# SSD and z with tokens on the partitions, decay exponents from one matmul, the norm by 128 tokens

## The chip, the cores and the metric

One core of a Trainium2 chip runs the whole kernel. The metric is the device time of one execution in microseconds (us). PE is the matrix engine, DVE the vector engine, ACT the scalar engine, POOL GpSimd, SP the engine whose queue issues most DMAs. The matrix engine's granted clock has two levels here, 1.2 and 2.4 GHz (0.50 and 1.00 in the profile).

## What is computed

One layer of a decoder for a prompt of 2048 tokens and 8 samples of 4 tokens, 1024 channels wide. The normed input goes through one projection; four groups of 256 channels (S5, attention, SSD, short convolution) work on its parts; each is normed, all four go through W_out, and a feed-forward net follows. The change is in the SSD group and in its gate z:

```python
def ssd_scan(x, a, bm, cm, h0):
    ...
    acum = jnp.cumsum(jnp.transpose(a.reshape(bsz, nc, chunk, H), (0, 3, 1, 2)), axis=-1)
    li = jnp.arange(chunk)
    lmat = jnp.exp(jnp.where(li[:, None] >= li[None, :],
                             acum[..., :, None] - acum[..., None, :], -jnp.inf))
    scores = jnp.einsum('bclhn,bcshn->bhcls', ch, bh) * lmat
    y_diag = jnp.einsum('bhcls,bcshp->bclhp', scores, xc)
    decay_states = jnp.exp(acum[..., -1:] - acum)
    states = jnp.einsum('bclhn,bhcl,bclhp->bchpn', bh, decay_states, xc)
    ...
    y_off = jnp.einsum('bclhn,bchpn,bhcl->bclhp', ch, new_states[:, :-1], jnp.exp(acum))
...
    y = y + d_skip.astype(F32)[:, None] * xs
    y = y.reshape(bsz, T, SSD_WIDTH).astype(z.dtype) * jax.nn.silu(z)
    return rmsnorm(y, norm_g), h_new, new_buf
```

The prompt has 16 chunks of 128 tokens, 4 heads of 64 channels, 2 groups of B and C, and a state of 128.

## The kernel before

**Stages.** The norm of the inputs and the first projections come first, then the dense products of the input projection with S5 and the samples' attention beside them (to 811 us). SSD's products with X follow from 838 to 1017 us, the products with W_out (`px<-w,cat`) from 1053 to 1310 us, and the feed-forward net takes the rest. The prompt's attention runs as filler beside the end of the dense part, SSD and W_out; its last product with V is at 1195.7 us.

**Order.** A scheduler fixes each engine's instructions in one row when the program is built; at run time an engine takes its row strictly in order. What is traced at an earlier priority is taken first where it is ready, so `run` traces SSD ahead of the attention, and the attention ahead of W_out. Tiles come from pools: a name with `bufs=n` has n slots, handed out in the order in which the program is traced, and a slot is free again when its last reader is done.

**Input projection.** `w_cols` lists the chunks of 128 columns in their order. `dense_xbc` makes xBC (6 chunks) and z (2 chunks, last) with channels on the partitions: for each chunk and block of 512 tokens `proj_feat` issues 24 products of 512 columns; `proj_tok` is its counterpart with tokens on the partitions, 24 products of 128 columns for each 128 tokens and chunk. Both go through `silu2` to `xbcD` in DRAM, 8 rows of channels.

**SSD.** `prepare(i)` makes what does not wait for the state: it loads `sxbc` (every second chunk) and `sac`, the cumulated log decays as a row for each head read by all partitions (L1058). It transposes x and B (`px<-cst,sxbc`), makes `sX`, `sXd`, `sBt`, two exponentials (`seA` L1071, `sE` L1076), where four DVE operations (L1075) subtract the column's sum, G = B C, its mask (`sGm` L1081), `sE` times `sGm` (L1085), and `sCe` on POOL (L1087). `advance(i)` makes y with channels on the partitions (`pd<-sE,sX`, `pd<-sCe,shT`), the state (`px<-sXd,sBt`, L1106, L1107), the skip by D (L1110) and the gate (L1112). `feat_norm_out` norms 256 tokens at once: squares (L983), sums by a product with ones, rsqrt, product back to all partitions, scale (L995), split to two fp16 parts in `cat`. The samples' SSD (`sample`) and the preparation of W_out's weights (`wo`, `w_out`, L171 and L178) are steps of the same loop.

**Attention.** For each block of 512 queries (j) and head, `attend` makes scores (`pb<-k,q`, `pb<-kbm,q`), an exponential to `P` (L874), two fp16 parts `ph` (L878) and `pl` (L881), and products with V (`pb<-v,ph`, `pb<-v,pl`); the maxima of scores are found ahead (L843). After four heads `fox_out` norms 128 tokens at a time: squares with the sum (L928) into `fo_ssq`, rsqrt on POOL (L145, L146) into `fo_rs`, scale (L931), two transposes (`pb<-cst,fo_on`), split (L465, L466), DMA to `cat`. A block's output `fo_o` has one buffer:

```python
                o = f1.tile([128, 4, 256], F32, name="fo_o")
...
        ssq = self.col("fo_ssq", bufs=4)
...
        rs = self.col("fo_rs", bufs=4)
```

`col` takes these two from the pool `small`, which the whole kernel shares.

Of the kernel before, what the change touches and what calls it, by code (L numbers as in the profile page):

```python
# [9 lines left out]
F32 = mybir.dt.float32  # L10
# [3 lines left out]
AF = mybir.ActivationFunctionType  # L14
# [3 lines left out]
T = 2048          # prompt tokens  # L18
NT = 16           # prompt token tiles
D = 1024  # L20
KT = 8
B = 8             # sample batches
TS = 4            # sample tokens per batch
# [4 lines left out]
BLOCKS = [(2, 3), (0, 1)]  # blocks of 512 tokens, by pass over the FFN's weights; the first pass takes the samples too  # L28
FC = 256          # hidden channels of a step of the FFN
PLAIN = ((0, 15), (1, 15))      # (pass, step) of the FFN that leave the vector engine to others: products down as they come  # L30
V_EARLY, V_LAG = 12, 4     # token tiles whose v is made beside the norm of the inputs, and how far behind it
# [5 lines left out]
def host_constants():  # L37
# [17 lines left out]
    # score rows (head, batch, token); pages on partitions (batch % 4, page)  # L55
# [8 lines left out]
    # rows (token group, batch parity, head, token) of the products with V  # L64
# [4 lines left out]
    c["m8"] = (r[:, None] - 64) // 2 == np.arange(4)[None, :]  # L69
    offs, cols, n = {}, [], 0  # L70
# [8 lines left out]
    return offs, np.ascontiguousarray(np.concatenate(cols, 1)), n0  # L79


C_OFFS, C_ARR, C_LATE = host_constants()
# [16 lines left out]
class K:  # L99
    """One step of the hybrid trunk on one core."""  # L100
# [9 lines left out]
    # ------------------------------------------------------------ helpers  # L110
# [6 lines left out]
    @contextmanager  # L117
    def banks(self, **tags):
        """the group of PSUM banks (x, d or b) that a tag stands for"""
        old, self.bank = self.bank, tags  # L120
        yield
        self.bank = old

    @contextmanager
    def priority(self, p):
        """the scheduler takes what is traced here as if it were traced at p"""
# [14 lines left out]
    def rsqrt(self, out, v, add, mul):  # L141
        """out = (v * mul + add) ** -0.5 on small tiles"""
# [5 lines left out]
    def pow2(self, out, v):  # L148
        """the power of two at or below v > 0"""
# [8 lines left out]
    def wprep(self, loads, kt, ncols, tag="w", st=None):  # L158
        """Load weights, scale them by a power of two that bounds the chunk's norm by 2**15,
        split into fp16 parts.  Returns tile [128, kt, 2, ncols], scale, 1/scale."""  # L160
# [8 lines left out]
    def split(self, hi, lo, x, sc):  # L169
        """fp16 parts of sc * x"""  # L170
# [3 lines left out]
    def wscale(self, st, junk, sc, inv, top):  # L174
        """the power of two that brings the norm of st to 2**top or below, and its inverse"""
# [2088 lines left out]
```

## Time and profile before

| what | value |
| --- | --- |
| runs | 2616.5, 2621.11, 2626.45 us; median 2621.11 us |
| profiled execution | span 2617.2 us, 50130 instructions |
| PE busy | 2431.6 us (93%) |
| DVE busy | 2050.2 us (78%) |
| ACT busy | 1308.3 us (50%) |
| POOL busy | 1246.8 us (48%) |

The span is the time from the first to the last recorded instruction of one profiled execution, and stands 3.9 us under the median of the runs. Shares are means over stages with different limits; they are read stage by stage below.

### The profile page before, as it was taken

How to read it: one execution, taken by the hardware profiler on the slowest of the kernel's cores; microseconds unless marked ns; L12 is line 12 of the kernel's file. 1: busy time of each engine (PE TensorE's matmuls, PEld its weight loads, DVE VectorE, ACT ScalarE, POOL GpSimd, SP SyncE). 2: the span in 40 equal slices, each digit the busy share in tenths (PEclk: the TensorE clock that was granted, in tenths of full speed). 3: DMA queues.
4: the chain of work that ended last, by engine and by line, in shares of the span. 5: the costliest groups of instructions: out<-in, count | busy, mean ns of one | idle time of the engine just before them, and what ended most of it. 6: DMA issues, size and time to landing. Idle time of an engine off the chain costs nothing.

```text
span 2617.2 us, 50130 instructions
## 1 busy us (share of the span) xinstructions
PE 2431.6 (93%) x19944; PEld 1628.7 (62%) x19944; DVE 2050.2 (78%) x3822; ACT 1308.3 (50%) x2376; POOL 1246.8 (48%) x1274
## 2 busy tenths in 40 slices
PE   6989999999988898999969999999998999999997
PEld 5875554444444666778956666666665666666664
DVE  5666667875565988665579998899998898999996
ACT  6444332033335566565365655655556554455554
POOL 3503122223113766454265565556656666666652
PEclk9999999999998989999989999999999999999999
DMA  6333416869724343436111121111126211121211
GB/s 189 93 75 93 90 38 215 305 253 331 229 84 149 109 136 96 129 108 227 52 41 49 49 65 49 49 49 49 62 81 232 96 49 49 65 65 49 65 33 65
DMA packets 205476, 282.27 MB, mean 108 GB/s; under 512 B 33765, under 2 KB 170082, under 8 KB 194970
## 3 DMA queue, kind: packets, MB, share of 16 engines
q1 hardware_dynamic: 195866, 211.44, 25.8%
q0 software_dynamic: 9376, 67.64, 7.1%
q8 instruction: 156, 2.56, 0.4%
q14 instruction: 78, 0.64, 0.1%
HBM read 221.90 MB, written 54.28 MB: 106 GB/s over the span
## 4 chain that ended last, share of the span: by engine, by line
PE 29%; DVE 12%; POOL 12%; ACT 5%; issue 3%; DMA 3%; POOLq 0%; DVEq 0%; ACTq 0%
PE pb L135 17%; PE px L135 11%; DVE x L2150 3%; DVE wu L172 2%; DMA ws<-in_w_up_dram 2%; DVE wd L172 1%; POOL ws L1996 1%; ACT wu L171 1%; POOL ws L1995 1%; POOL ws L1998 1%; POOL ws L1997 1%; ACT wd L171 1%; POOL ws L2022 1%; POOL ws L2024 1%; ACT wdT L171 1%
## 5 line engine op out<-in xcount | busy, mean ns | idle before, releaser
L135 PEld LDWEIGHTS <-wu 128*128 128x128 f16 x5376 | 528.9, 99 | 229.6 <-issue 43.4
L2150 DVE SCALAR_TENSOR_TENSOR x<-pb,ff,x 128x512 f32<-128x512 f32 x840 | 592.0, 740 | 26.5 <-PE pb L135 22.7
L135 PE MATMUL px<-hn,wu 128*128 128x256 f16 (+1 forms) x3072 | 427.6, 276 | 20.4 <-ACT fr L2057 10.0
L135 PE MATMUL px<-xT,w 128*128 128x512 f16 (+1 forms) x2160 | 416.3, 343 | 2.4 <-ACT da L721 2.1
L135 PEld LDWEIGHTS <-ht 128*128 128x128 f16 x2712 | 264.0, 98 | 226.4 <-issue 25.8
L135 PE MATMUL pb<-wdT,ht 128*128 128x512 f16 x1440 | 376.7, 379 | 10.4 <-DVE x L2150 8.1
L135 PE MATMUL pb<-wd,ht 128*128 128x512 f16 x1272 | 334.8, 379 | 10.4 <-DVE x L2150 10.4
L135 PE MATMUL pb<-hn,wu 128*128 128x256 f16 (+1 forms) x2304 | 302.1, 277 | 16.8 <-DVE x L2150 7.5
L135 PEld LDWEIGHTS <-w 128*128 128x128 f16 x2352 | 186.6, 99 | 207.8 <-issue 30.8
L881 POOL TENSOR_TENSOR pl<-P,ph 128x512 f16<-128x512 f32 (+3 forms) x160 | 173.7, 1095 | 171.0 <-ACT ph L878 75.7
L171 ACT ACTIVATE wu<-ws,wsc 128x1024 f16<-128x1024 f32 (+1 forms) x128 | 129.5, 1036 | 140.5 <-POOL ws L1998 64.3
L172 DVE SCALAR_TENSOR_TENSOR wu<-ws,wsc,wu 128x1024 f16<-128x1024 f32 (+1 forms) x128 | 168.9, 1330 | 20.6 <-ACT wu L171 20.2
L135 PE MATMUL px<-w,cat 128*128 128x256 f16 x1536 | 181.9, 272 | 3.3 <-DMA cat<-cat 3.2
L135 PEld LDWEIGHTS <-cat 128*128 128x128 f16 x1536 | 148.2, 98 | 27.6 <-DMA cat<-cat 3.7
L874 ACT ACTIVATE P<-pb,nck,cc 128x512 f32<-128x512 f32 (+3 forms) x160 | 112.4, 709 | 82.3 <-PE pb L135 77.3
L2102 ACT ACTIVATE ht<-fr 128x1024 f16<-128x1024 f32 (+1 forms) x60 | 64.1, 1068 | 141.8 <-POOL fr L2108 141.8
L2021 POOL TENSOR_TENSOR ws<-ws 128x512 f32<-128x512 f32 x30 | 39.0, 1299 | 198.7 <-DVE wd L172 198.7
L2105 POOL TENSOR_TENSOR ht<-fr,ht 128x512 f16<-128x512 f32 (+1 forms) x60 | 72.2, 1204 | 114.1 <-ACT ht L2104 107.8
L2079 ACT ACTIVATE fr<-fr 128x256 f32<-128x256 f32 (+1 forms) x192 | 77.2, 413 | 98.6 <-DVE fr L2060 98.0
L843 DVE TENSOR_REDUCE mx<-pb 128x1 f32<-128x512 f32 (+3 forms) x160 | 94.3, 604 | 36.2 <-PE pb L135 35.5
L135 PE MATMUL px<-w,xT 128*128 128x128 f16 (+1 forms) x1632 | 101.7, 224 | 17.1 <-DVE xT L397 8.2
L135 PEld LDWEIGHTS <-xT 128*128 128x128 f16 (+1 forms) x1904 | 104.4, 100 | 20.1 <-DVE xT L397 12.0
(698 smaller groups left out, 4720.9 us busy)
## 6 DMA issues: line engine op xcount, KB each, us to landing
ws<-in_w_up_dram SPq DMA_DIRECT2D x32, 1024.0 KB
ws<-in_w_down_dram SPq DMA_DIRECT2D x32, 1024.0 KB
ws<-in_w_in_dram SPq DMA_DIRECT2D x22, 512.0 KB
x<-in_x_prompt_dram SPq DMA_DIRECT2D x16, 512.0 KB
xbc<-dc SPq DMA_DIRECT2D x32, 256.0 KB
sxbc<-xbc SPq DMA_DIRECT2D x8, 1024.0 KB
x<-in_x_prompt_dram SPq DMA_DIRECT2D x8, 1024.0 KB
cat<-cat SPq DMA_DIRECT2D x32, 256.0 KB
```

What stands on the lines that cost most here:

```text
L135: self.nc.tensor.matmul(out, lhsT, rhs, start=start, stop=stop, skip_group_check=True)
L171: self.nc.scalar.activation(hi, x, AF.Copy, scale=sc)
L172: self.nc.vector.scalar_tensor_tensor(lo, x, sc, hi, op0=OP.mult, op1=OP.subtract)
L843: nc.vector.tensor_reduce(mx[:, ii, jb:jb + 1], s[:, :n], axis=AX.X, op=OP.max)
L874: nc.scalar.activation(P[:, :n], s[:, :n], AF.Exp, bias=nck[:, j, h, kt:kt + 1], scale=cc[:, h // 2:h // 2 + 1])
L881: (nc.gpsimd if 1 else nc.vector).tensor_sub(pl[:, :n], P[:, :n], ph[:, :n])
L1995: nc.gpsimd.tensor_add(A22, A21, A22) # S1
L2021: nc.gpsimd.tensor_sub(B11, B12, B11)
L2079: nc.scalar.activation(x, x, AF.Relu)
L2102: nc.scalar.activation(ht[:, o:o + m, 0, :], x, AF.Copy)
L2105: nc.gpsimd.tensor_sub(ht[:, 0:2, 1, :], C[:, 0:2, :], ht[:, 0:2, 0, :])
L2150: nc.vector.scalar_tensor_tensor(o, p, f, o, op0=OP.mult, op1=OP.add)
```

## The change

**z.** Its two chunks of weights come ahead of xBC's. For each of 16 tiles of 128 tokens `proj_tok` makes both chunks (48 products of 128 columns), two ACT copies scale them, `silu2` follows, and a DMA writes 128 KB to `zD`. `xbcD` keeps 6 rows.

**SSD.** The exponents of the decays come from one product with K=5 (`RL`: the sums as one row of 512 and as four rows of 128, each beside constant rows of 1 and −1; 512 columns) and a second product that adds the causal mask (`cnegb` and the identity), both into one PSUM tile, and ACT makes one exponential of 512 columns from it. One DVE operation of 512 columns multiplies it by G. y has tokens on the partitions: the skip by D is a product with a diagonal matrix `Dd`, C times the state goes to its own half of the bank, and the product with X has 64 columns for each head. DVE multiplies the second half by the decay of the token (`acu`) and adds the first, POOL multiplies by z. Two small DMAs into `RL` and one of 128 KB (`sz`) stand for each chunk in place of `sac`.

**Norm.** `fox_out` with `g=2` takes each chunk of 128 tokens one chunk late, with `fo_ssq`, `fo_rs` from the same rings as the attention, in place of `feat_norm_out` on 256.

```diff
--- before.py
+++ after.py
...
+    z = np.zeros((128, 640))
+    z[1:5, :512] = -1.0 * (np.arange(512)[None, :] // 128 == np.arange(4)[:, None])
+    z[0, 512:] = 1.0
+    rows = z
...
-                       [C_X + 128 * c for c in range(6)] + [C_Z, C_Z + 128])
+                       [C_Z, C_Z + 128] + [C_X + 128 * c for c in range(6)])
...
+        for i in range(NT):
+            p = self.ps("mm", [128, 2, 128])
+            acc = post.tile([128, 2, 128], F32, name="zacc", tag="b")
+            for c in range(2):
+                self.proj_tok(p[:, c, :], self.xs_tok(i), Wz[c][0], 0, 128)
+            for c in range(2):
+                nc.scalar.activation(acc[:, c, :], p[:, c, :], AF.Copy, scale=hz[:, c:c + 1])
+            e = post.tile([128, 2, 128], F32, name="ze", tag="c")
+            self.silu2(e, acc, e)
+            nc.sync.dma_start(self.zD[i], e.rearrange("p c n -> p (c n)"))
...
-    def fox_out(self, pool, o, n, i, bank="t"):
+    def fox_out(self, pool, o, n, i, bank="t", g=1):
...
-            nc.sync.dma_start(self.catD[1][i // 4][:, :, :, (i % 4) * 128:(i % 4) * 128 + 128], cat)
+            nc.sync.dma_start(self.catD[g][i // 4][:, :, :, (i % 4) * 128:(i % 4) * 128 + 128], cat)
...
+            z = p2.tile([128, 256], F32, name="sz")
+            nc.sync.dma_start(z, self.zD[i])
+            rl = RL[ii]
+            nc.sync.dma_start(rl[0:1, 0:512], acD[4 * i:4 * i + 4, :].rearrange("(o h) p -> o (h p)", o=1))
+            nc.sync.dma_start(rl[1:5, 512:640], acD[4 * i:4 * i + 4, :])
+            E_ = self.ps("s", [128, 4, 128])
+            self.mm(E_, rl[:, 512:640], rl[:, 0:512].rearrange("p (h n) -> p h n", h=4), start=True, stop=False)
+            self.mm(E_, self.cnegb, self.identb[:, None, :].to_broadcast([128, 4, 128]), start=False, stop=True)
+            E = p2.tile([128, 4, 128], F32, name="sE")
+            nc.scalar.activation(E, E_, AF.Exp)
...
-            eA = p2.tile([128, 4, 128], F32, name="seA")
-            nc.scalar.activation(eA, ac, AF.Exp)
-            E = p2.tile([128, 4, 128], F32, name="sE")
...
-            for h in range(4):
-                nc.vector.tensor_scalar(E[:, h, :], ac[:, h, :], nac[:, i * 4 + h:i * 4 + h + 1], 0.0, op0=OP.add, op1=OP.min)
-            nc.scalar.activation(E, E, AF.Exp)
-            G = self.ps("s", [128, 4, 128])
+            G = self.ps("s", [128, 2, 128])
...
+            Ev = E.rearrange("p (g h) n -> p g h n", g=2)
+            nc.vector.tensor_mul(Ev, Ev, G[:, :, None, :].to_broadcast([128, 2, 2, 128]))
...
+            y = self.ps("o", [128, 2, 256])
+            for c in range(2):
+                self.mm(y[:, 0, c * 128:(c + 1) * 128], xbc[:, c, sl], Dd[:, c, :], start=c == 0, stop=False)
+            if i > 0:
+                for g in range(2):
+                    self.mm(y[:, 1, g * 128:(g + 1) * 128], xbc[:, 4 + g, sl], hT[:, 2 * g:2 * g + 2, :], start=False, stop=True)
             for h in range(4):
...
+                self.mm(y[:, 0, h * 64:(h + 1) * 64], M[:, h, :], X[:, h, :], start=False, stop=True)
...
+                nc.vector.tensor_mul(yt.rearrange("p (h d) -> p h d", d=64), y[:, 1, :].rearrange("p (h d) -> p h d", d=64),
+                                     acu[:, i, :, None].to_broadcast([128, 4, 64]))
+                nc.vector.tensor_add(yt, yt, y[:, 0, :])
+                nc.gpsimd.tensor_mul(yo, yt, z)
+            return hN, yo
...
+            if old is not None:
+                self.fox_out(p2, old, 128, i - 1, "t", 2)
...
-        self.feat_norm_out(p1, *norm)
+        self.fox_out(p2, yo, 128, NT - 1, "t", 2)
```

**ACT in the middle of SSD.** Ahead of the change ACT's row there is SSD's exponentials (L1071, L1076) with the attention's exponentials and fp16 parts (`P`, `ph`) between:

```order
L1076 ACTIVATE sE<-sE 128x512
L878 ACTIVATE ph<-P 128x256
L874 ACTIVATE P<-pb,nck,cc 128x128
L878 ACTIVATE ph<-P 128x128
L874 ACTIVATE P<-pb,nck,cc 128x512
L1071 ACTIVATE seA<-sac 128x512
```

In the changed kernel the same place (`syo` is y times z, `px` the PSUM tile of the exponents) reads:

```order
L470 ACTIVATE fo_cat<-px,gcat 128x128 x2
L952 ACTIVATE fo_on<-syo,fo_rs 128x256
L1096 ACTIVATE sE<-px 128x512
L949 ACTIVATE fo_on,fo_ssq<-syo 128x256
L1106 ACTIVATE sBt<-px 128x256
L952 ACTIVATE fo_on<-syo,fo_rs 128x256
```

The attention's lines are gone from there. On PE, 908 of its products stood between the last product of the input projection and the last of SSD's with X; now there are none. From there to its last product with V stood 1260 of its products, and stand 2167 now.

**ACT at the attention's first norms** (`fo_on<-fo_o`; `fo_o` is a block's output). Before, they stand at the end of the dense part, next to the samples' gate (`accS`, `qe`), the convolution's norm (`fn_cat`) and SSD's first small tile (`av`):

```order
L744 ACTIVATE accS<-px,hz 128x32
L976 ACTIVATE qe<-accS 128x256
L928 ACTIVATE fo_on,fo_ssq<-fo_o 128x256 x2
L931 ACTIVATE fo_on<-fo_o,fo_rs 128x256
L465 ACTIVATE fn_cat<-fn_sq_6703,gcat 128x256 x2
L1015 ACTIVATE av<-av 128x4
```

Now they stand at the end of SSD, behind its next to last norms (`fo_on<-syo`):

```order
L1106 ACTIVATE sBt<-px 128x256
L176 ACTIVATE w<-ws,w_sc 128x8x256
L470 ACTIVATE fo_cat<-px,gcat 128x128 x3
L949 ACTIVATE fo_on,fo_ssq<-syo 128x256
L949 ACTIVATE fo_on,fo_ssq<-fo_o 128x256 x2
L470 ACTIVATE fo_cat<-px,gcat 128x128
L952 ACTIVATE fo_on<-syo,fo_rs 128x256
L470 ACTIVATE catS<-fn_sq_11058,gcat 128x32 x2
L952 ACTIVATE fo_on<-fo_o,fo_rs 128x256 x2
```

They have moved past the whole of SSD.

**PE behind the attention's last product with V** (`xn` are rows of the feed-forward net's normed input, to be transposed). Before:

```order
L135 MATMUL pb<-v_3_10468,pl 128x65
L135 LDWEIGHTS cat
L135 MATMUL px<-w,cat 128x256
```

After:

```order
L140 MATMUL pb<-v_3_11115,pl 128x65
L144 MATMUL pb<-cst,fo_on 128x128 x8
L144 MATMUL pb<-cst,xn 128x128 x12
L140 MATMUL pd<-w_ss,ones 128x1
L144 MATMUL pb<-cst,xn 128x128 x12
L140 LDWEIGHTS cat
L140 MATMUL px<-w,cat 128x256
```

Behind this place stand 910 of the 1536 products with W_out before, and 378 now, all of the last block of tokens; the attention's last transposes (`fo_on`) now stand ahead of them.

## Rows read from the trace of the kernel before

**Rows 1.** The page: busy time of each engine, share of the span, instructions.

```profile
PE 2431.6 (93%) x19944; PEld 1628.7 (62%) x19944; DVE 2050.2 (78%) x3822; ACT 1308.3 (50%) x2376; POOL 1246.8 (48%) x1274
```

**Rows 2.** Busy time by stretch (us), count, PE clock, DMA share, GB/s.

```profile
core 0: us, PE busy (x) PEld busy (x) DVE busy (x) ACT busy (x) POOL busy (x), PEclk, DMA share, GB/s
811.40:837.70 26.30, 17.53 (x136) 11.72 (x135) 15.62 (x44) 18.50 (x43) 10.00 (x15) 0.74 0.68 202
837.70:1016.50 178.80, 158.08 (x1503) 115.18 (x1501) 161.09 (x386) 107.95 (x203) 127.83 (x155) 0.90 0.38 117
1016.50:1054.00 37.50, 27.79 (x320) 18.02 (x319) 28.79 (x53) 21.77 (x37) 21.37 (x23) 0.91 0.44 133
1054.00:1195.00 141.00, 140.30 (x1634) 110.60 (x1632) 88.85 (x153) 95.65 (x162) 79.83 (x84) 1.00 0.38 124
```

**Rows 3.** DVE by line, 837.7 to 1016.5: busy, mean ns, idle before, releaser.

```profile
L843 DVE TENSOR_REDUCE mx<-pb 128x1 f32<-128x512 f32 (+3 forms) x61 | 36.0, 601 | 4.5 <-PE pb L135 4.3
L1075 DVE TENSOR_SCALAR sE<-sac,nac 128x128 f32<-128x128 f32 x64 | 28.9, 492 | 4.7 <-DMA sac<-acD 2.7 <-PE pd L135 2.1
```

**Rows 4.** PE timeline, z's two forms of product: start, us, instruction.

```profile
122.03 2.84 PE L135 MATMUL px<-w,xT 128*128 128x128 f16 x48 [1.29 <-DVE v L562]
283.16 5.14 PE L135 MATMUL px<-xT,w 128*128 128x512 f16 x23
```

**Rows 5.** PE timeline in the middle of SSD: start, us, instruction.

```profile
910.10 0.22 PE L135 MATMUL pb<-v,ph 128*128 128x65 f16 x2
910.16 0.19 PE L135 MATMUL pb<-v,pl 128*128 128x65 f16 x1
910.18 0.38 PE L135 MATMUL pb<-k,q 128*128 128x512 f16 x1
910.40 0.38 PE L135 MATMUL pb<-kbm,q 74*128 74x512 f16 x1
910.62 0.61 PE L135 MATMUL px<-sXd,sBt 128*128 128x128 f32 x4
911.07 0.97 PE L135 MATMUL px<-ones,fn_sq 128*128 128x1 f32 x8
```

**Rows 6.** ACT by line, 837.7 to 1016.5, columns as in rows 3.

```profile
L1076 ACT ACTIVATE sE<-sE 128x512 f32<-128x512 f32 x16 | 10.0, 626 | 8.4 <-DVE sE L1075 8.3
L171 ACT ACTIVATE w<-ws,w_sc 128x2048 f16<-128x2048 f32 x3 | 6.0, 1999 | 3.6 <-DVE w_sc L186 3.6
L1211 ACT ACTIVATE qh0T<-px 128x512 f32<-128x512 f32 x4 | 2.3, 582 | 1.9 <-PE pb L135 1.9
```

**Rows 7.** Timeline of one attention norm at 813 us, ACT and POOL.

```profile
813.50 0.42 ACT L928 ACTIVATE fo_on<-fo_o 128x256 f32<-128x256 f32 x1 [1.49 <-DVE fo_o L892]
813.83 0.19 ACT L928 ACTIVATION_READ_ACCUMULATOR fo_on<-fo_o 128x1 f32 x1
814.10 0.19 POOL L145 TENSOR_SCALAR fo_rs<-fo_ssq 128x1 f32<-128x1 f32 x1 [0.46 <-ACT fo_on L928]
814.37 0.56 POOL L146 TENSOR_TENSOR fo_rs<-fo_rs,mhalf 128x1 f32<-128x1 f32 x1
814.96 0.51 ACT L931 ACTIVATE fo_on<-fo_o,fo_rs 128x256 f32<-128x256 f32 x1 [0.55 <-POOL fo_rs L146]
```

**Rows 8.** Timeline, two transposes of a scaled norm on PE.

```profile
1200.80 0.38 PE L139 MATMUL pb<-cst,fo_on 128*128 128x128 f32 x2
```

**Rows 9.** Busy time by stretch where SSD begins, columns as in rows 2.

```profile
844.00:848.00 4.00, 2.15 (x11) 1.44 (x12) 4.00 (x12) 0.93 (x3) 2.28 (x4) 0.50 0.53 161
848.00:852.00 4.00, 4.00 (x34) 2.48 (x32) 4.00 (x10) 1.90 (x4) 3.24 (x5) 0.68 0.06 22
```

**Rows 10.** Timeline behind the last product with V: output, first DMA.

```profile
1196.46 0.43 DVE L892 TENSOR_TENSOR fo_o<-pb,rl 128x256 f32<-128x256 f32 x1
1209.31 1.57 SPq L942 DMA_DIRECT2D cat<-fo_cat  x2
```

**Rows 11.** The chain that ended last: a read of cat.

```profile
1046.00 7.44 DMA cat<-cat
```

## What the trace leads one to expect

> **What bounds the kernel now.** I read the page first: PE is busy 93% of the span [rows 1], so what decides is where PE stands still, and whether work that moves lands where PE has room. The busy time by stretch [rows 2] shows four places that the change touches. In the lead-in to SSD (811.4 to 837.7) PE works 17.5 of 26.3 us. In SSD (837.7 to 1016.5) it works 158.1 of 178.8 us, part of it at the lower clock (0.90 in the mean), beside a DVE that is busy 161.1 us. The seam that follows has 9.7 us of idle PE. From 1054 to 1195 PE has nothing left to give: 140.3 busy of 141.0 us at full clock. The second view, DVE by line over SSD's stretch [rows 3], shows who fills that engine: the attention's maxima (36.0 us) and SSD's own subtractions (28.9 us). So SSD's stretch is long since two programs share it, and the attention uses PE's gaps there.
>
> The third view is the order of instructions. In the changed kernel no instruction of the attention stands between the last product of the input projection and the end of SSD, on any engine. The names say why. `fox_out` takes `fo_ssq` and `fo_rs` from rings of four slots, handed out in the order of the program. SSD is traced ahead of the attention and now takes 16 turns in these rings, so the norms of the attention's first query block get their slots from SSD's last ones. `fo_o` has one buffer, which stays full until then, so the second query block has nowhere to put its output, and the attention stops. This is a wait that the change adds without naming it: behind it stand 908 products of PE with their maxima, exponentials and splits.
>
> **The sum, part by part.**
>
> z: 48 products of 128 columns took 2.84 us and 23 of 512 columns 5.14 us [rows 4], .0592 and .2235 us for one. Before, 192 of the long kind: 42.9 us. After, 768 of the short kind: 45.4 us. **+2.5 us.** ACT's copies, tanh and the DVE product lie beside the dense products of the next tile; if PE waited half a microsecond for each of 16 tiles it would be 8 more, so 0 to 10.
>
> The lead-in: xBC's chunks now end the projection, not z's, so SSD's first load comes closer behind its data, while 100 of the attention's products leave the stretch. Its idle PE, 8.8 us, bounds a gain; a late first load bounds a loss by a few us. I take 0, within −6 and +4.
>
> SSD alone. With the attention gone, a chunk is a chain through all engines, since PE's row has the transposes of one chunk's norm ahead of the next chunk's y, and the exponents of a later chunk behind that y, while ACT's row has that exponential ahead of the square of the norm:
> - exponents on PE: no row shows a product with K=5. An f32 product shows as two passes, and four passes of 128 columns start .45 us before what comes next (910.62 to 911.07), .11 each [rows 5]. 512 columns are taken as eight such, .90 us, and the mask as one product of 512 columns, .22 (910.18 to 910.40): 1.12. Between .5 (at the pace of the mask's) and 2.2 (all at the lower clock), for 16 chunks −10 to +18.
> - the exponential, .63 [rows 6]; the square and its sum's read, .42 + .19, two operations on POOL, .19 + .56, the scale, .51 [rows 7]; two transposes, .38 [rows 8]
> - C times the state, four passes, .45; the products with X, eight passes, .90 [rows 5]
> - seven hand-overs between engines of .05 each, as from ACT's read to POOL and on [rows 7]: .35.
>
> That is 5.7 us, 91 for 16 chunks. On ACT, in the same row, stand the five preparations of W_out's weights, 2.0 each, and four copies of the samples' state, 2.3 together [rows 6]: 12.3. The entry runs at the lower clock as now: .50 and .68 over 4 us each lose 3.3 us [rows 9]. The first chunk has nothing beside it, some 4 us by the same prices. The stretch becomes 111 us in place of 178.8 [rows 2]: **−67.8 us**. From below it is held by PE's own work for a chunk: these products (1.12 + .38 + .45 + .90), four more transposes (.76), and the skip, G and the state (.45 each) make 4.96, so 79 us. DVE loses the 28.9 us of subtractions and the attention's maxima [rows 3] and is below that.
>
> The attention held back: the 908 products are, by the order, 182 of 512 columns, 26 of 384, 26 of 256, 83 of 128 and 591 of 64 or 65. A product of 512 columns takes .22, the narrower ones in proportion to their columns, and those of 65 .03 (910.10 to 910.16 for two) [rows 5]: 40.0 + 4.3 + 2.9 + 4.6 + 17.7 = 69.5 us. They land beside the products with W_out, where PE has .7 us of idle time in 141 [rows 2], so they cost their full price: **+69.5 us**, up to 5% more, since nothing there can absorb them. The cover that was lost is SSD's stretch, where the same products filled gaps.
>
> The end of the attention: the last block's `cat` needs the last four norms. Now they run beside 910 remaining products with W_out. After the change the row of PE has only 378 left there, all of that last block, so PE waits for them. From the output (1196.46) to the issue of the first pair of transfers is 12.9 us [rows 10], and a read of `cat` behind its write took 7.4 us where the chain shows one [rows 11]; 32 transposes for the feed-forward net, some 4 us, lie beside. 20.3 − 4 is 16; without the hold-ups of the products in between a little less: **+15 us**, between 0 and 22.
>
> The seam from SSD to what follows has W_out's products waiting for their first `cat` now (9.7 us idle [rows 2]); afterwards the attention is ready to fill it, and it has its own start to make. 0.
>
> The sum is 2.5 − 67.8 + 69.5 + 15 = +19.2 us. The profiled execution has a span of 2617.2 us, 3.9 below the median of the runs; put on the median, the time is 2640 us. Run to run, 0.5% (13 us, so 2608 to 2634) is about what a measurement of this kernel can tell from no change.
>
> **Rivals.**
>
> The last norms are hidden: PE finds the transposes for the feed-forward net and earlier blocks' remainders so placed that the gap is 0 to 4 us. For it speaks that a norm takes 2 us from its square to the end of its scale [rows 7], and four in a row overlap; against it, that the order leaves nothing but the last block's products there. The sum is then +4 to +8: about 2627.
>
> Faster: the hand-overs overlap, and SSD alone runs at PE's own load, 79 us. For it speaks that a chunk's preparation does not wait for the state, so it can fill the waits of the norm; against it, that each engine takes its row strictly in order, with the norm inside. SSD's term becomes −99.8, the sum −12.8: 2608. The point from which it decides is a stretch of SSD of 92 us, where the sum is 0; below 79 it would be faster by more than 0.5%, and with 80 and a shorter end as well.
>
> Slower still: the lower clock holds through SSD. For it speaks the entry: 0.50 in four microseconds in which PE worked 2.15 us, and 0.68 in the next four, all busy [rows 9]. Against it, that PE alone with SSD works 4.96 of 5.7 us in a chunk by the prices above, though no row shows it so. At 1.2 GHz PE's 4.96 us of a chunk become 9.9, more than the chain's 5.7 + 2.85, so PE sets the pace: 16 chunks take 160 us. The sum is then 2.5 − 18.8 + 69.5 + 15 = +68: 2689.
>
> The Trainium skill, page "TensorE: Matmul & The Clock Gate", section "HAM oscillation — how this bites in real kernels", describes the same as a rule: pauses of the matrix engine bring the lower clock back, again and again in a kernel that works in short bursts. By that rule this rival would hold in every chunk; the trace agrees for the entry (0.50 behind a stretch of waiting), and shows no stretch in which SSD runs alone.
>
> That the change doesn't hold the attention back is no rival: the order is fixed when the program is built.
>
> **Chances and range.** The chain with the attention held back: .55, with its own range 2620 to 2660, of which .38 is slower by over 0.5% and .17 within. The hidden end: .18, within. PE's own load: .15, of which .13 faster by over 0.5% (with some of the end hidden too) and .02 within. The lower clock: .12, slower. Together faster .13, within .37, slower .50. The time is that of the likeliest, 2640. The range goes from 2608, where the faster rival begins, to 2676, which leaves out most of the lower clock's case: about 2 in 10 are outside.
>
> **What would show it.** In the changed profile: no `P`, `ph` or `mx` between the last dense product and SSD's last y (right by the order; what counts is the length of that stretch: 111 us, 79 or 160, with the granted clock beside it). ACT's idle time in it should end with `sE` and `fo_rs`. Between SSD's end and the attention's last product with V, PE should be full, at some 70 us of work more than before. Behind that product PE should show one wait of about 15 us for `cat`. From the first product of the feed-forward net to the end nothing should change. The prediction is wrong if PE shows idle time beside W_out's products (the moved work then fills it for less than its price), if SSD's chain waits at a place that I hold to be hidden (the loads of `sz` and `RL`, the product with G), or if the dense part gains or loses more than its 2.5 us.

## The result, and the profile after

The changed kernel takes 2712.64 us in the median of 4 runs (2708.28 to 2725.43), the kernel before 2623.78 (2616.5 to 2632.14): a ratio of 1.0347, interval 1.0312 to 1.0382. It is slower by 89 us, where +19 was forecast and 2676 was the top of the range. The page of its profiled execution, the counterpart of [rows 1]:

```profile
span 2712.8 us, 51398 instructions
PE 2481.6 (91%) x20508; PEld 1684.4 (62%) x20508; DVE 2016.3 (74%) x3735; ACT 1324.8 (49%) x2449; POOL 1222.6 (45%) x1265
```

PE has 50 us more busy time than before, and 46 us more without work. Busy time by stretch, columns as in [rows 2], cut at the last product of the input projection (820.8), SSD's first and last product with X (868.4, 994.1), the first product with W_out (1012.1), the attention's last with V (1345.8) and the first product of the feed-forward net (1411.0):

```profile
core 0: us, PE busy (x) PEld busy (x) DVE busy (x) ACT busy (x) POOL busy (x), PEclk, DMA share, GB/s
820.80:868.40 47.60, 20.63 (x75) 13.39 (x75) 13.69 (x38) 11.90 (x24) 2.70 (x4) 0.53 0.45 136
868.40:994.10 125.70, 114.92 (x648) 89.52 (x646) 62.24 (x151) 51.17 (x119) 43.96 (x80) 0.79 0.31 92
994.10:1012.10 18.00, 8.85 (x46) 5.39 (x46) 10.09 (x30) 10.74 (x33) 6.71 (x14) 0.59 0.56 139
1012.10:1345.80 333.70, 311.75 (x3575) 234.79 (x3575) 205.11 (x374) 197.93 (x337) 172.19 (x179) 0.95 0.31 104
1345.80:1411.00 65.20, 55.53 (x463) 48.49 (x464) 37.85 (x80) 33.18 (x62) 18.88 (x22) 0.90 0.27 83
```

The trace before, cut at the same marks:

```profile
811.30:846.00 34.70, 21.64 (x175) 14.78 (x174) 21.14 (x59) 23.01 (x52) 15.35 (x23) 0.77 0.71 211
846.00:1015.70 169.70, 153.27 (x1458) 111.91 (x1458) 154.87 (x368) 103.33 (x194) 121.68 (x146) 0.90 0.36 112
1015.70:1053.50 37.80, 28.09 (x322) 17.89 (x319) 29.09 (x55) 21.97 (x38) 22.17 (x24) 0.91 0.42 128
1053.50:1195.80 142.30, 141.59 (x1643) 111.60 (x1644) 90.15 (x156) 95.79 (x163) 80.41 (x84) 1.00 0.38 124
1195.80:1312.50 116.70, 115.06 (x1204) 104.17 (x1202) 62.77 (x119) 46.53 (x80) 26.18 (x30) 1.00 0.39 128
```

So the projection's end came 9.5 us later, the entry to SSD took 12.9 us more, SSD 44.0 less, the seam 19.8 less, the stretch to the attention's end 191.4 more, the rest up to the feed-forward net 51.5 less, and the feed-forward net 2.9 less: +95.6 us, the difference of the spans. The three stretches behind SSD together grew by 120 us.

These marks are not quite those of the prediction. Its stretch of SSD begins at 837.7 us, where SSD's first transposes stand; the first product with X comes at 846.0. In the changed kernel the first transposes stand at 862.4 us. By the prediction's marks SSD took about 46 us less, and the lead-in ahead of it 15 us more.

What fills these 120 us shows in the view of PE's waits from 1012 to 1346 us (engine, line, what it waited for: us, times, longest), and in busy time by pieces of 40 us:

```profile
PE pb L144 <- ACT fo_on L952: 12.6, 5, 9.3
```

```profile
1040.00:1080.00 40.00, 39.89 (x439) 31.20 (x438) 29.66 (x53) 24.37 (x39) 17.76 (x18) 1.00 0.36 124
1080.00:1120.00 40.00, 34.31 (x315) 25.13 (x313) 25.98 (x46) 23.35 (x48) 17.97 (x22) 0.87 0.49 168
1120.00:1160.00 40.00, 40.00 (x461) 31.36 (x460) 27.13 (x49) 22.88 (x38) 21.59 (x24) 1.00 0.23 75
1160.00:1200.00 40.00, 39.43 (x429) 29.62 (x427) 29.79 (x50) 23.81 (x36) 20.73 (x20) 1.00 0.30 110
1200.00:1240.00 40.00, 24.87 (x220) 15.51 (x218) 24.01 (x42) 23.32 (x48) 16.62 (x20) 0.74 0.55 186
1240.00:1280.00 40.00, 40.00 (x473) 29.72 (x470) 22.06 (x43) 24.47 (x39) 23.14 (x23) 1.00 0.09 29
```

PE is full but for two holes, 5.7 us near 1100 and 15.1 us near 1220, and the granted clock falls in each (.87, .74). There PE waits for the norm of a query block (`fo_on`), near 1100 also for the rows of the feed-forward net (2.3 us), and once more for `fo_on` at 1346. By the order, the transposes of these three norms stand behind 390 to 396, 780 and 1158 products with W_out, just past one, two and three blocks' 384: all that the finished blocks allow is spent each time. The wait of 9.3 us near 1220 is not the norm alone: DVE and ACT worked on the feed-forward net's input (`tt`, `hnr`) ahead of the block's output and its norm, and in two other kernels with the attention held (below: the hold alone, and z last) the same wait is 3.5 us.

The count of the 120 us: PE's busy time behind SSD is 376.1 us against 284.7, +91.4, of which 69.5 were the priced products; its idle time is 40.8 against 12.1, +28.7. Of the idle time, 21.2 us were added ahead of the attention's last product with V (22.0 against .7) and 8.0 behind it (9.7 against 1.6). The rest of the busy time, 21.9 us, is in size mostly the clock's: in the five spells at .50 between 994 and 1411 us PE was busy 40.2 us, in the one before 5.4, and if all of that work takes half the time at 1.00, the clock cost 20 us against 2.7. That is at most 17 of the 21.9 us; the other 4 or more are not explained.

### The profile page after: what moved, and what is told of

Read it like the earlier page. It is cut to its first block, busy times and chain, and to the rows that moved or that the text cites. A ratio compares the mean times of both kernels' runs of the same rounds, so it can differ in the third digit from the quotient of the medians.

```text
span 2712.8 us, 51398 instructions
## 1 busy us (share of the span) xinstructions
PE 2481.6 (91%) x20508; PEld 1684.4 (62%) x20508; DVE 2016.3 (74%) x3735; ACT 1324.8 (49%) x2449; POOL 1222.6 (45%) x1265
## 4 chain that ended last, share of the span: by engine, by line
PE 48%; DVE 16%; POOL 12%; DMA 9%; issue 6%; ACT 6%; SPq 2%; POOLq 0%; DVEq 0%; ACTq 0%
PE pb L140 23%; PE px L140 22%; DVE x L2177 3%; DVE wu L177 2%; PE pd L140 2%; DMA ws<-in_w_up_dram 1%; DVE wd L177 1%; DMA kp<-in_cache_k_dram,ptK 1%; POOL ws L2023 1%; PE pb L144 1%; DMA zD<-ze 1%; ACT wu L176 1%; POOL ws L2022 1%; DMA ws<-in_w_in_dram 1%; POOL ws L2025 1%
## 5 line engine op out<-in xcount | busy, mean ns | idle before, releaser
L140 PE MATMUL px<-xT,w 128*128 128x512 f16 (+1 forms) x1968 | 367.5, 338 | 0.3 <-DVE qk_hl L621 0.3
L140 PEld LDWEIGHTS <-w 128*128 128x128 f16 x2160 | 169.4, 99 | 177.3 <-issue 15.9
L140 PE MATMUL px<-w,cat 128*128 128x256 f16 x1536 | 195.2, 275 | 3.6 <-DMA cat<-cat 3.6
L140 PEld LDWEIGHTS <-xT 128*128 128x128 f16 (+1 forms) x2672 | 150.1, 100 | 30.7 <-issue 17.4
L140 PE MATMUL px<-w,xT 128*128 128x128 f16 (+1 forms) x2400 | 152.1, 224 | 18.5 <-DVE xT L402 8.4
```

Source lines behind the costliest of these rows:

```text
L140: self.nc.tensor.matmul(out, lhsT, rhs, start=start, stop=stop, skip_group_check=True)
```

## Experiments

Theory A says that the shared rings hold the attention and that this is most of the loss. Theory B says that the new SSD and z are slow in themselves. Each ratio below is to runs of the kernel before that were taken beside it; the medians of those lay between 2622 and 2630 us, so a difference of a few us between two experiments is read from the ratios.

**SSD's own small tiles.**

```diff
-        ssq = self.col("fo_ssq", bufs=4)
+        ssq = self.col("fo_ssq", bufs=4) if g == 1 else pool.tile([128, 1], F32, name="so_ssq")
...
-        rs = self.col("fo_rs", bufs=4)
+        rs = self.col("fo_rs", bufs=4) if g == 1 else pool.tile([128, 1], F32, name="so_rs")
```

> The changed kernel, with fo_ssq and fo_rs of SSD's norms taken from SSD's own pool; nothing else differs. By the order 130 of the attention's products stand ahead of SSD's first y and 962 in SSD, none in the changed kernel. Theory A (the shared rings are the main cost: the moved work, a gap of PE at the end of each query block, and the lower clock behind each gap): the products return to SSD's stretch, which grows to about 165 us; between SSD's end and the feed-forward net PE has no gaps again. The dense part's 9.5 us and the later entry to SSD (13 us) stay. Time 2638 us, 2620 to 2655. Theory B (SSD and z in the new form are slow in themselves, by f32 products and the lower clock, and the attention's place matters little): 2690 us or more.

Measured 2630.29 us, ratio to before 1.0 (0.9982 to 1.0018). By the ratios the whole loss is gone with two small tiles (by the medians 82 us of it, with the kernel before at 2629 us here). So with tiles of its own the new form stands level with the kernel before. Its busy time by stretch from SSD's first y to the feed-forward net:

```profile
889.10:1077.10 188.00, 184.33 (x1621) 136.19 (x1620) 131.78 (x300) 126.62 (x268) 113.28 (x157) 0.89 0.30 87
1077.10:1103.90 26.80, 21.06 (x252) 13.16 (x249) 21.80 (x46) 19.88 (x39) 21.36 (x23) 1.00 0.42 110
1103.90:1183.50 79.60, 76.08 (x923) 59.59 (x924) 43.20 (x77) 50.45 (x82) 48.10 (x47) 0.96 0.37 122
1183.50:1337.80 154.30, 154.22 (x1569) 139.84 (x1566) 82.35 (x145) 58.99 (x97) 28.13 (x37) 1.00 0.45 150
```

The holes behind SSD are gone, but for 9 us in 261 up to the feed-forward net, and with them the lower clock, but for .96 in one stretch. SSD's stretch took 188 us in place of the 165 expected: PE is busy in 184 of them at .89, so PE now bounds the new SSD; DVE, busy 155 us of 170 before, has room.

**The hold alone, in the kernel before.** 32 small copies, read by nobody, take SSD's turns in the rings:

```diff
             nc.gpsimd.tensor_mul(yo[:, :, sl], xbc[:, 6:8, sl], yt)
+            for name in ("fo_ssq", "fo_rs"):
+                nc.vector.tensor_copy(self.col(name, bufs=4), yt[:, 0, 0:1])
```

> The kernel before, with the hold alone: after each of SSD's 16 chunks two DVE copies of 128x1 take a turn in each of the rings fo_ssq and fo_rs; the copies are read by nobody (32 copies, about 2 us of DVE). By the order no product of the attention stands in SSD any more, and 378 products with W_out behind its last product with V, as in the changed kernel. Theory A: SSD alone in its old form shortens by some 50 us, and the stretch behind it grows by the 120 us that it grew in the changed kernel: about 2690 us, 2660 to 2720. Theory B: within 2600 to 2640, since the old SSD and z are kept.

Measured 2689.03 us, 1.0235 (1.0218 to 1.0252). In this kernel everything is old but the turns in the rings and the 32 copies:

```profile
839.80:969.70 129.90, 102.44 (x645) 84.56 (x644) 90.32 (x266) 45.17 (x79) 58.16 (x86) 0.66 0.38 111
1000.80:1325.10 324.30, 303.24 (x3492) 229.86 (x3492) 204.45 (x362) 190.52 (x325) 163.59 (x172) 0.96 0.30 99
```

Old SSD alone takes 130 us, and the stretch with W_out up to the attention's end 324 where [rows 2] had 141. Theory B is out.

**What stops the attention.** My prediction named `fo_o`. By the order, a second buffer of `fo_o` alone brings no product back into SSD. The held norms' transposes also have turns in the five PSUM banks of tag b, ahead of the next block's scores. (The order has 0 products in SSD with two buffers of `fo_o`, 492 to SSD's last y with the norms' PSUM tile elsewhere, 1146 with both.) Two kernels take the stops away one after the other; in both the norms themselves still wait:

```diff
-                    self.fox_out(f2, o[:, ii, :], 128, 4 * j + ii, "b")
+                    self.fox_out(f2, o[:, ii, :], 128, 4 * j + ii, "d")
```

> The changed kernel, rings of fo_ssq and fo_rs still shared; only the PSUM tile of the attention's norms is taken from tag d in place of b. Theory C (the hold has two stops: the transposes of the held norms have their turns in the ring of five PSUM banks, tag b, which the next block's scores need; and behind that fo_o with its one buffer): with the first stop gone 354 of the attention's products stand ahead of SSD's first y and 138 in SSD by the order, 492 of the 1092 that own rings brought back. At the same price for each, .45 of the 82 us between the changed kernel and the one with own rings: 2675 us, 2660 to 2692. Theory D (what costs is the gaps of PE at the ends of the query blocks, not how many products are held): the gaps behind the later blocks stay, 2695 to 2715.

Measured 2680.11 us, 1.0223 (1.0193 to 1.0253). Then, beside that edit, a second buffer of `fo_o`; to make room, `P`, `ph` and `pl` get three buffers in place of four:

```diff
-                o = f1.tile([128, 4, 256], F32, name="fo_o")
+                o = f1.tile([128, 4, 256], F32, name="fo_o", bufs=2)
```

> As the kernel with the norms' PSUM tile from tag d, and fo_o with two buffers; for the room P, ph and pl have three buffers in place of four. Theory C: with both stops gone 1146 products stand ahead of SSD's last y by the order, and 995 products with W_out behind the attention's last; the time is that of own rings, 2630 us, 2622 to 2645, though the norms themselves still wait for SSD's. If fewer buffers of the exponentials bind, or if the held norms alone cost: 2650 or more.

Measured 2643.48 us, 1.0063 (1.0043 to 1.0084). Both came inside theory C's ranges, which were worked out from the count of products that each frees. By the ratios to before, 17 us above the kernel with own tiles are left (.0063 of 2624): fewer buffers or the held norms, not told apart.

**z's place.** Four kernels. z last again, by tokens, with the last norms of the short convolution in its loop; first with the own tiles:

```diff
-                       [C_Z, C_Z + 128] + [C_X + 128 * c for c in range(6)])
+                       [C_X + 128 * c for c in range(6)] + [C_Z, C_Z + 128])
...
+            if i % 8 == 7:
+                self.sc_norm(6 + i // 8)
```

> The changed kernel with SSD's own small tiles, and z again at the end of the input projection (still by tokens), with the last two norms of the short convolution inside z's loop. Theory A, with the step that the entry to SSD is late because the norms and the last chunk of xBC have no products left beside them: the entry shortens by some 13 us and z's start has its cushion back, so 2615 us, 2595 to 2635. If the entry is set by SSD's first loads and not by these norms: as the kernel with own tiles alone, within 5 us. Theory B: above 2670.

Measured 2616.27 us, 0.9954 (0.9935 to 0.9972). Then with the rings still shared:

> The changed kernel with z at the end of the input projection (by tokens, with the last two norms of the short convolution in its loop), and the rings still shared. By the order the attention is held as in the changed kernel. Theory A: only the entry and the dense part gain, 13 to 20 us of the 91: 2695 us, 2685 to 2705. If z's place had brought the whole loss: 2630 or below. If the entry is set by SSD's first loads: no change, 2706 to 2720.

Measured 2674.36 us, 1.0189 (1.0169 to 1.0209): 38 us under the changed kernel, twice what was expected. By the marks the projection ends 9.0 us earlier (811.8), the entry is 19.8 us shorter and SSD 8.3. With the attention free z's place is worth 14; that it counts for more with the attention held goes with the order, which then leaves the entry none of the attention's products. By the ratios the hold costs 62 us with z last, as in the kernel before, and 91 with z first.

z first and the norms early, with own tiles:

```diff
+            if i % 8 == 7:
+                self.sc_norm(i // 8)
...
-            self.sc_norm(c)
+            self.sc_norm(c + 2)
```

> The changed kernel with own small tiles for SSD's norms and z first, as the change has it; only the norms of the short convolution come two steps earlier, the first two inside z's loop and the rest beside xBC's chunks, so that none is left behind the last chunk. With z first and the norms late the time was 2630 us, with z last 2616. If the late entry to SSD comes from the norms left behind the last product: 2616 us, 2608 to 2622. If it comes from z's place alone (the last chunk of xBC has no product left beside its convolution, and z's start has no cushion): 2625 to 2635.

Measured 2626.2 us, 1.0014 (1.0 to 1.0029), as with the norms late: it is the place, not the norms. Last, the kernel before with z's place changed alone (old form, norms 6 and 7 behind the loop):

```diff
-        for c in range(8):
+        for c in (6, 7, 0, 1, 2, 3, 4, 5):
...
-            self.sc_norm(c)
+            if c < 6:
+                self.sc_norm(c)
+        self.sc_norm(6)
+        self.sc_norm(7)
```

> The kernel before, with z's place alone changed: its two chunks ahead of xBC's, in the old form with channels on the partitions, and the last two norms of the short convolution behind xBC's last chunk, as the change has them. If the place is what costs some 14 us in the entry and the dense part: 2636 us, 2630 to 2645. If it costs only together with the new form of z: 2617 to 2628.

Measured 2639.93 us, 1.0066 (1.0044 to 1.0088): 17 us for the place in the old form too.

**SSD alone.** With the attention held and z last it took 117.4 us, more than the 111 forecast. Busy time of its two halves of eight chunks (cut at the ninth chunk's exponents):

```profile
839.60:890.30 50.70, 48.51 (x322) 37.90 (x320) 26.32 (x64) 20.11 (x59) 21.29 (x41) 0.94 0.34 100
890.30:957.00 66.70, 61.01 (x329) 48.53 (x329) 37.42 (x91) 30.32 (x60) 20.69 (x39) 0.76 0.35 100
```

First, useless products of PE to hold its clock (G gets a PSUM tile of twice the size for them):

```diff
+            for _ in range(8):
+                self.mm(G[:, 2:4, :], self.cnegb, self.identb[:, None, :].to_broadcast([128, 2, 128]))
```

> The changed kernel with z last (2674 us, the attention still held), and in each chunk of SSD eight bf16 products of 256 columns more, into a free half of the PSUM tile of G, read by nobody: .9 us of PE at full clock. If the lower clock sets SSD's length when it runs alone (117 us for 16 chunks at a granted clock of .83): the clock rises, the stretch falls to 108 us or below, and the time to 2660 to 2670 in spite of the added work. If the chain over the engines sets it whatever the clock: between no change (the products fit the waits) and 14 us longer, 2674 to 2690.

Measured 2693.82 us, 1.0269 (1.0243 to 1.0295). That is 4 us above the range of the second case. The stretch grew by 15 us, the price of the added products, at .85:

```profile
836.30:968.50 132.20, 120.27 (x768) 95.99 (x767) 64.10 (x157) 51.98 (x120) 45.32 (x80) 0.85 0.30 89
```

So more work on PE did not give the clock back, and PE's row had no room for it in a chunk. The weights' preparation moved to the first half:

```diff
-            if i in (10, 12, 13, 14):
+            if i in (2, 3, 4, 5):
```

> The kernel with the attention held and z last (2674 us), whose first eight chunks of SSD took 50.7 us (6.3 each, granted clock .94) and the last eight 66.7 (8.3 each, .76). The preparation of W_out's weights, which stands beside the chunks from the tenth on, is moved to chunks 2 to 5. If it is what slows the second half: the slow half is now the first, near 65 us, and the second near 52. If the samples' steps of the same loop slow it, which stay: the second half keeps 60 us or more. In both cases the time is within 8 us of 2674.

Measured 2693.37 us, 1.0263 (1.0233 to 1.0293): outside the 8 us that I allowed (13 us in SSD, and 7 in the feed-forward net, which the edit does not touch). Both halves were slow, 62 and 68 us, so each branch came true in part. From one chunk's first product with X to the next one's, the fourth, fifth and sixth step took 11.1, 11.2 and 12.3 us where they had taken 6.6, 5.9 and 6.1, and the last fell from 11.4 to 6.7: these go with the weights. The eighth, twelfth and thirteenth stayed slow, 11.8, 10.5 and 12.6 us (11.5, 10.9 and 12.7), though the weights had left the last two: these go with the samples, whose products stand in PE's row there. In the changed kernel's SSD the samples and the weights have these groups on PE (busy time, mean ns):

```profile
L140 PE MATMUL px<-qBt,qXb 32*128 32x128 f32 x32 | 5.5, 321 | 0.7 <-DVE shT L1132 0.7
L140 PE MATMUL pd<-qCe,qh0T 128*64 128x4 f32 x64 | 4.9, 207 | 0.0
L144 PE MATMUL px<-cst,qh 128*128 128x128 f32 x16 | 2.7, 291 | 2.8 <-DMA qh<-in_state_ssd_dram 2.3 <-DVE shT L1132 0.4
L140 PE MATMUL pd<-w_ss,ones 128*128 128x1 f32 x8 | 1.5, 255 | 0.3 <-DVE syt L1140 0.3
```

Last, the samples' steps and the weights both behind the loop:

```diff
-            next(sample, None)
-            if i in (10, 12, 13, 14):
-                next(wo)
+        self.fox_out(p2, yo, 128, NT - 1, "t", 2)
         for _ in sample:
             pass
-        self.fox_out(p2, yo, 128, NT - 1, "t", 2)
+        for _ in wo:
+            pass
```

> The kernel with the attention held and z last (2674 us, SSD's products with X over 117.4 us); the samples' steps and the preparation of W_out's weights are moved out of the loop and stand behind its last chunk. If these two set the excess of SSD's stretch over the predicted 91 us of chunks: sixteen chunks of 6.0 us, 96 us from first to last y, at a granted clock of .95 or more. If the clock falls in SSD alone whatever stands beside it: 110 us or more, at .85 or less. The total is no test of this (the moved work stands behind SSD): 2665 to 2700.

Measured 2666.22 us, 1.0165 (1.0124 to 1.0206). SSD's stretch, its two parts, and PE's timeline of the exponents' product, once a chunk:

```profile
838.81:935.41 96.60, 85.50 (x496) 66.71 (x496) 42.55 (x102) 37.21 (x102) 38.51 (x74) 0.87 0.31 87
838.80:857.90 19.10, 19.10 (x74) 15.04 (x73) 5.25 (x12) 4.51 (x12) 4.63 (x9) 0.50 0.21 63
857.90:935.40 77.50, 66.40 (x426) 51.67 (x425) 37.31 (x91) 32.69 (x90) 33.88 (x65) 0.96 0.33 93
```

```profile
860.79 1.12 PE L140 MATMUL px<-RL 5*128 5x512 f32 x2 [0.36 <-DVE shT L1131]
866.61 1.12 PE L140 MATMUL px<-RL 5*128 5x512 f32 x2 [0.36 <-DVE shT L1131]
872.43 1.12 PE L140 MATMUL px<-RL 5*128 5x512 f32 x2 [0.36 <-DVE shT L1131]
878.25 1.12 PE L140 MATMUL px<-RL 5*128 5x512 f32 x2 [0.36 <-DVE shT L1131]
```

96.6 us, a chunk every 5.82 where the clock is full, and 8.4 to 8.5 at .50. The loop's companions, the samples' steps and the weights, made the 21 us above that. The clock matched neither branch (.87): it is low for the first 19 us and falls at two later places, but not for much of the time.

**The exponents' product in bf16.** The sums are split into three bf16 parts, K=15 in place of 5; own tiles, z last:

```diff
-        RL = [p1.tile([5, 640], F32, name=f"RL{k}") for k in range(2)]
+        RL = [p1.tile([15, 640], BF, name=f"RL{k}") for k in range(2)]
...
+        for k in range(3):
+            nc.vector.tensor_copy(acP[:, k, :], acT)
+            if k < 2:
+                nc.vector.tensor_sub(acT, acT, acP[:, k, :])
```

> The kernel with own small tiles and z last (2616 us), with the sums split into three bf16 parts, so that the product of the exponents is one bf16 product with K=15 in place of the f32 one with K=5. An f32 product of 512 columns took 1.0 us on PE in SSD at full clock, a bf16 one .22: 12 us less PE work in a stretch where PE is busy 174 of 182 us. If PE's own work bounds SSD with the attention beside it: 2604 us, 2597 to 2610. If another engine or the chain bounds it: 2612 to 2620.

Measured 2598.78 us, 0.9906 (0.9885 to 0.9926), the fastest of all; by the ratios 13 us under the same kernel with the f32 product. SSD's stretch in the f32 form (first) and the bf16 form:

```profile
868.10:1050.30 182.20, 173.86 (x1504) 127.96 (x1503) 125.22 (x291) 118.54 (x256) 107.11 (x150) 0.89 0.31 90
```

```profile
861.00:1021.80 160.80, 152.95 (x1475) 117.24 (x1474) 124.10 (x286) 114.82 (x255) 106.96 (x149) 0.95 0.35 102
```

21 us less in that stretch, in an execution that is 7 us faster than the median of its kernel. The f32 product took 1.05 us to the next one's start and the bf16 one .31, 12 us for 16 chunks; the granted clock rose beside it, which accounts for the rest in size, without a run that shows it. The same edit with the attention held:

> The attention held (shared rings), z last, as in the kernel of 2674 us, but with the exponents' product in bf16 (K=15). With SSD alone: if PE's own row sets the chunk, as the added products suggest (.88 us more a chunk made 15 us more), .8 us less a chunk makes 12 us less: SSD's stretch 105 us, the time 2661 us, 2655 to 2667. If the f32 product also holds the clock down (with the attention beside SSD the granted clock went from .89 to .95 with this edit, and the stretch lost 21 us): the clock rises from .83 to .9 or more and the time is 2645 to 2655. If other engines set the chunk: 2668 to 2678.

Measured 2673.0 us, 1.019 (1.0157 to 1.0224): no gain beside 2674, the case in which other engines were to set the chunk. Where the clock is full its chunks come every 5.2 to 5.5 us in place of 5.9 to 6.0 and the first half took 45.4 us for 50.7, but the second half with its companions took 70.5 us at .69, for 66.7 at .76. So in this trace what PE's shorter row gains in the first half is lost in the second, at a lower clock; why the clock is lower there is not shown.

## Why the prediction was wrong

The mechanism was found, its price was too small. The attention was held, by the two rings, as the order showed: own tiles give the whole loss back, and the hold alone costs the old kernel 60 us. The sum was short by 76.4 us (19.2 against 95.6). It failed in the sizes of four terms, all in the same direction, and in one that it did not have, the clock: 35.6 us behind SSD, 23.8 in SSD, 12.9 in the lead-in and 7.0 in z, less 2.9 in the feed-forward net.

- **"The end of the attention", +15.** The end itself was +8.0 us of idle time, inside its range. The step that failed took W_out's products as cover that runs out once, at the last block, and held PE to be full up to there. The cover runs out at the end of each block: W_out's products for a block wait for that block's norm, so the held attention drags them along, and PE found nothing else at 1100, 1220 and 1346 us. The stretch ahead of the last product with V, with the earlier blocks' ends priced at nothing, added 21.2 us; +28.7 us of idle time were measured in all. The seam, priced at 0, kept its idle time (9.2 us, 9.7 before).
- **The clock behind SSD** was priced at nothing. It fell in each hole, and that is at most 17 of the 21.9 us of busy time above the 69.5. The holes and the low clock go together in the kernel with own tiles. With the point before, this is the 35.6 us.
- **"The attention held back", +69.5**, agrees with the +91.4 us of PE's busy time as far as the clock's share explains the rest. The stop was not `fo_o` alone, as written, but first the PSUM banks; the two runs show both.
- **"SSD alone", −67.8.** A chunk costs 5.82 us where 5.70 was worked out, and 4.97 of it is PE's work, where 4.96 was: with the chunks by themselves the stretch is 96.6 us. That 5.70 came so near is luck: it was a chain through four engines, 2.85 us of it on PE, while the chunk is PE's own row with two short waits, .36 us for the state (`shT`) and .49 for the reader of the last y, and none for the norm. What failed is the 12.3 us for W_out's weights and the samples. They were priced by ACT's time alone; their products on PE, 14.6 us in the rows above, were held at nothing. With the clock they cost 21 us in the kernel with z last, and about 29 in the changed one (125.7): PE is busy 29.4 us more there than with the chunks by themselves, and by what the clock lacks to 1.00 (114.92·.21 against 85.50·.13) some 13 of that are the clock's.
- **The lead-in, 0 within −6 and +4, was +12.9** (about +15 by the prediction's marks), and **z, +2.5, was +9.5.** Both come from z's place (17 us in the old form, 14 with own tiles): with z last by tokens and the attention held the projection ends at 811.8 us, .5 behind the old one, so the new form of z costs nothing that shows. The order shows it: before, z's products stood behind the last chunk of xBC and its norms, and now nothing dense does. A late first load was taken to cost a few us. In the changed kernel SP's row has the last of the convolution's norms ahead of SSD's first load, one of these stores waits 7.9 us for its data, at a clock of .50, and PE then waits for the load:

```profile
844.19 9.03 SPq L1024 DMA_DIRECT2D cat<-fn_cat  x2
857.70 0.39 SPq L1085 DMA_DIRECT2D sxbc<-xbc  x1
862.42 1.11 PE L144 MATMUL px<-cst,sxbc 128*128 128x128 f32 x4 [5.55 <-DMA sxbc<-xbc]
```

The rival of the lower clock gave 2689, nearest to the result, but by another way: SSD ran at .79, not .50, and took 126 us, not 160. The granted clock fell in every hole (.87, .74, .90). The Trainium skill, page "TensorE: Matmul & The Clock Gate", section "HAM oscillation — how this bites in real kernels", says that pauses of the matrix engine bring the lower clock back; these rows agree, and the .89 in a stretch where PE is busy 184 of 188 us is not explained by it. That the lower clock would hold in every chunk did not come true: with the chunks by themselves it held for the first 19 us (.50), and behind them the granted clock was .96, with PE's two waits in each chunk. The rival of PE's own load, and that of a hidden end, did not occur.

What stays open is how much of SSD's and the entry's time is the clock in itself: no run held the clock up with the same work.

## What to carry to other kernels

A helper that is called from a second place also takes turns in the first caller's rings; where tiles are handed out in program order, a small tile with four slots can order two independent programs one behind the other. The order of instructions shows it before any run, and the remedy is a tile of its own. When work is moved behind a seam, what matters is not its own price alone but whether the work that used to cover its waits now depends on it: count the cover at each wait, not at the last one.

## What the runs showed of the hardware

- An f32 product with K=5 and 512 columns is followed after 1.05 us, a little more than eight passes of the full K by [rows 5] (.90); in bf16 with K=15 after .31.
- With SSD and the attention together PE was busy 98% of 188 us at a granted clock of .89; with fewer f32 products .95; eight bf16 products more in a chunk of SSD alone only .83 to .85.
- A busy PE alone did not bring the full clock: with the chunks by themselves PE was busy 19.10 of 19.10 us from SSD's first product with X on, and the granted clock stayed at .50 (1.2 GHz) for all of it.
